# Twenty-four gate projections spread over four stages, and the third triangular solve moved into the scan

## The chip, the core and the metric

The kernel runs on one core of a Trainium2 chip. A core has a matrix engine (TensorE, PE in the profile; its weight loads are PEld), a vector engine (VectorE, DVE), an activation engine (ScalarE, ACT), a general engine (GpSimd, POOL) and a queue that issues most transfers (SyncE, SP). Each engine works through its own list of instructions in order, and semaphores make one wait for another. The metric is the time on the device in microseconds (us) for one launch. The kernel before takes 1673.54 us, the median of three runs (1671.61 to 1678.89).

## The reference

One layer of a hybrid backbone on 512 latent and 256 context tokens of width 1024, all in float32. One input projection `w_in` feeds three token mixers; their outputs are weighted by gates, projected and followed by a convolutional feed-forward part. What matters here:

```python
proj = h @ w_in      # split into q/k/v, z, a/b, hyena, lru x, lru y, gates
# A. gated DeltaNet: 8 heads, chunks of 64 tokens, two directions
t_inv = triangular_solve(eye + m, eye, left_side=True, lower=True)
def step(state, inp):                      # 4 context chunks, then 8 latent ones
    v_new = u_i - w_i @ state
    o_i = q_i @ state + a_i @ v_new
    state = state * d_i + k_i @ v_new
o = rms_norm(o, norm_g) * silu(z)          # z: 8 column blocks of proj
# B. Hyena (long convolution), C. RG-LRU, 8 blocks of 128 channels, two directions
r = sigmoid(blockdiag(x, w_a) + b_a); i = sigmoid(blockdiag(x, w_x) + b_x)
log_a = -8 * r * softplus(-lam)
h = linear_scan(exp(log_a), sqrt(-expm1(2 * log_a)) * (i * x), h0)
out = (h_f + flip(h_b)) * gelu(p_y)
# merge: three sets of 8 gate blocks
g_dn, g_hy, g_lru = split(sigmoid(p_gate))
merged = g_dn * (o_dn @ w_proj_dn) + g_hy * (o_hy @ w_proj_hy) + g_lru * (o_lru @ w_proj_lru)
```

The z blocks and the three sets of gates are 32 equal projections of the latent tokens, 1024 x 128 weights each. Their results are kept in DRAM until they are needed, so 24 of them (z, g_dn, g_hy; kinds 0, 1 and 2 in the kernel) can be computed anywhere between the normalised input and the work behind the scan.

## The kernel before

Every float32 product that matters is done as three products of rounded parts. `load_w` (L165) loads a 128 x 1024 weight tile (L168), splits it into a high part (L157 on POOL or L155 on ACT) and a low part (L160 on DVE or POOL), and `mm3` (L172 to L175) issues three matmuls for each of eight slices of the width. A gate on 512 tokens is thus 24 matmuls of 128x512, a sigmoid or silu on ACT (L574) and a store to the DRAM tensor `gated` (L575). Loads and stores share SP's queue.

The program has these stages, with their times in the trace of before:

- *RG-LRU* (101 to 340 us): eight blocks `g`. Each has the projection of the next block's input (`lru_in`, with the copies and the short convolution on L484 to L487), the eight small gate products and their sigmoids (`lru_gates`, L518 and L519 on ACT, L520 on DVE), four tanhs (L524, L525), one gate of kind 3, `lru_decay` (two exponentials L532 on ACT; L534 on DVE, L535 on POOL, a square L536 on ACT, L537 on DVE, a square root L539 on ACT), `lru_scan` (L542 to L547 on DVE), `lru_y` (a projection, L555 to L558), and `lru_out`, which adds and multiplies on POOL (L562, L563) and splits the result with L155 on ACT. Sigmoid and tanh, the exponential and the square root are in different tables of ACT, so ACT loads a table (ACT_TABLE_LOAD) where the function changes.
- *Merges, queries* (340 to 447): `lru_merge(h)` for seven values of h, each a projection of the RG-LRU output times a gate, between the DeltaNet's queries. Then the keys and the chunks' Gram matrices (447 to 540).
- *First two solves* (540 to 650): each `solve` inverts triangular blocks. Two transposes prepare its buffers (L819); an inner loop of 31 steps, two DVE instructions each (L827, L829), solves 32x32 blocks; transposes (L837, L839) put them back; 32x32 matmuls on TensorE (L853, L857) with copies on ACT complete the 64x64 inverses; the results go to the DRAM tensor `wad`. `run` weaves the two solves' steps with a work list of values and gates in turn, one item every third step.
- *Third solve* (650 to 743): `solve_second`, for the chunks that the scan reaches from its step 7 on, woven with the rest of the list.
- *Scan* (743 to 948): twelve steps, four on context and eight on latent chunks. A step loads its chunk (v, `wa`, kd), multiplies the state (L1005), subtracts (L1009), applies the inverse (L1015), and updates the state (L1023, L1028); between a step's two parts and behind it stands a gap. Half a gate goes into each of the 24 gaps. After some steps `mod_part` multiplies a tile of `w_mod` on DVE (L1052, L1054), and `mod_sum` sums it up.
- *Rest* (948 to 1675): Hyena, output projections, feed-forward.

A list scheduler orders each engine's instructions from the program, with the items under `tc.high_priority()` ahead. The order of an engine is therefore not always the order of the code.

Of the kernel before, what the change touches and what calls it, by code (L numbers as in the profile page):

```python
# [17 lines left out]
P = 128  # L18
# [55 lines left out]
def tile_block(ctx: ExitStack, tc: tile.TileContext, I: dict, out: bass.AP, dbg=None, upto=99):  # L74
    nc = tc.nc
# [496 lines left out]
    def gate_store(z_, m, pg):  # L572
        th = ur([P, NL])
        act(th, pg, GATES[z_][1])  # L574
        load(gated[z_, m], th)  # L575
# [25 lines left out]
    NFILL = 12  # L601
# [28 lines left out]
    for g in range(8):  # L630
# [4 lines left out]
        gate(3, g)  # L635
        lru_decay([g], [bufs])
# [89 lines left out]
    for h in range(1, NH):  # L726
        lru_merge(h)
        if h < 6:
            sqs.append(query(h + 2))
        if h < 7:  # L730
            query_out(h, sqs[h])
        if h > 1:
            for i, d in pairs[2 * h - 4:2 * h - 2]:
                decays(i, d)
# [76 lines left out]
    def solve(dirs, M, NX_, tmr, eng):  # L811
# [31 lines left out]
        for half in range(2):  # L843
            zp = dn([P, 16, 32])
            rp = dn([P, 16, 32])
            for c in range(2):
# [3 lines left out]
                ci = slice((1 - d) * 32, (1 - d) * 32 + 32)  # L850
                for a in range(16):
                    e = half * 16 + a
                    mmul(zp[pi, a, :], M[pj, e, ci], Wu[pj, e, :], start=True, stop=True)  # L853
                act(Z[pi, half * 512:half * 512 + 512], zp[pi].rearrange("p a b -> p (a b)"), AF.Copy)
                for a in range(16):
# [12 lines left out]
    def solve_second():  # L868
        yield from solve((0, 1), M3.rearrange("p t c h i -> p (t c h) i"),
                         [at(180 + 4 * i, [P, 32, 32]) for i in range(2)], ring(1, seq(188, 1, 2)), "dve")  # L870
# [53 lines left out]
    fill = [(z_, m) for z_ in range(3) for m in range(8)]  # L924
    EVERY, NW1 = 3, 12
# [10 lines left out]
    gates = [lambda f=f: gate(*f, "act", "pool") for f in fill[:NFILL]]  # L936
    work = [w_ for p_ in zip(values, gates) for w_ in p_] + values[len(gates):] + gates[len(values):]
    run([solve_first(0), solve_first(1)], work[:NW1])
    run([solve_second()], work[NW1:])
# [15 lines left out]
    mm = Banks([0])  # L955
    o = at(60, [P, 4, NH, P])
    S = [at(84 + 4 * d, [P, NH, P]) for d in range(2)]
    war = ring(4, seq(92, 4, 4))
# [6 lines left out]
    def chunk_loads(s, lat):  # L965

        v, kd, wa = vr([P, NH, P]), kdr([P, NH, P]), war([P, 2 if lat else 1, NH, 64])
# [88 lines left out]
    def mod_sum(q):  # L1056
        if q in (1, 2):
            mp = mm([P, 8])
# [3 lines left out]
        else:  # L1062
            row, brow = wr([1, D]), wr([1, D])
            load(brow, I["b_mod"][:, (2 + q) * D:(3 + q) * D])
            for b in range(2):
                mp = mm([1, 512])
# [4 lines left out]
    def gate_halves(z_, m):  # L1071
# [4 lines left out]
        gate_store(z_, m, pg)  # L1076
# [3 lines left out]
    halves = (None for z_, m in fill[NFILL:] for _ in gate_halves(z_, m))  # L1080
    ngap, FBM = 2 * (24 - NFILL), 1
    gap = 0
    for s_ in range(12):
# [3 lines left out]
        for part, _ in enumerate(step(s_)):  # L1087
            gap += 1
            for _ in range(gap * ngap // 24 - (gap - 1) * ngap // 24):
                next(halves)  # L1090
        for k in range(4) if s_ % 3 < 2 else ():
            mod_part(s_ // 3, s_ % 3 * 4 + k)
    assert next(halves, 1) == 1
# [515 lines left out]
```

## Time and profile before

| | us |
|---|---|
| runs of before (median of three) | 1671.61 / 1673.54 / 1678.89 |
| the profiled execution | 1676.85 |
| its span, first to last instruction | 1675.1 |
| TensorE busy | 1529.7 (91%) |
| DVE busy | 1195.7 (71%) |
| ACT busy | 615.7 (37%) |
| POOL busy | 589.3 (35%) |

The profile is of one execution; the page gives its busy times, a row of 40 slices of the span, the queues and the costliest groups of instructions. The trace behind it is asked for stretches of time (busy time of each engine, granted TensorE clock, DMA share), timelines (each instruction with the idle time before it and what ended it), waits and lines. A granted clock of 1.00 is the upper level of TensorE, 2.4 GHz, and 0.50 the lower, 1.2 GHz. In a stage, what counts is the wait that ends last there; a busy share over the whole span is a mean over stages with different limits.

### The profile page before, as it was taken

What the parts mean: (1) busy time and instruction counts of PE and PEld (TensorE: products, weight loads), DVE (VectorE), ACT (ScalarE), POOL (GpSimd) and SP (SyncE); (2) the same over time, 40 slices, a digit from 0 to 9 for tenths busy, and PEclk for the clock granted to TensorE, in tenths of its full rate; (3) what the DMA queues carried; (4) which work ended last, traced back from release to release, by engine and by line L of the source; (5) the groups of instructions that cost most, each with busy time, mean ns of one, the idle gap of its engine ahead of it and who ended that gap; (6) DMA issues with size and microseconds to landing.
All of it is one profiled execution on the core that took longest, in us unless ns stands there. A gap on an engine that the chain in (4) does not pass through costs nothing. (4 is left out here: it accounts for less than half of the span.)

```text
span 1675.1 us, 23659 instructions
## 1 busy us (share of the span) xinstructions
PE 1529.7 (91%) x9176; PEld 1258.0 (75%) x9176; DVE 1195.7 (71%) x1752; ACT 615.7 (37%) x1011; POOL 589.3 (35%) x401
## 2 busy tenths in 40 slices
PE   6899888889999899887999889999999999999998
PEld 2677777767887777775788678787888788888876
DVE  6877888756656997834666375777766899989873
ACT  4367787734553232320111330333222433333311
POOL 4653534325444360312434114222321233334441
PEclk9899999999999896878899999999999999999999
DMA  9432222335344332577888736322462223232331
GB/s 343 162 107 82 76 76 81 103 104 175 127 126 125 110 101 74 173 211 206 233 227 244 253 109 231 107 88 84 162 207 64 68 96 97 92 101 98 104 113 50
DMA packets 93056, 225.66 MB, mean 135 GB/s; under 512 B 9963, under 2 KB 30699, under 8 KB 92176
## 3 DMA queue, kind: packets, MB, share of 16 engines
q1 hardware_dynamic: 92112, 217.86, 41.6%
q0 software_dynamic: 832, 6.29, 0.9%
q8 instruction: 72, 1.18, 0.3%
q14 instruction: 40, 0.33, 0.1%
HBM read 190.45 MB, written 33.66 MB: 134 GB/s over the span
## 5 line engine op out<-in xcount | busy, mean ns | idle before, releaser
L173 PE MATMUL bank<-region,region 128*128 128x512 f32 (+1 forms) x2032 | 761.8, 376 | 28.9 <-DVE region L487 6.8
L175 PE MATMUL bank<-region,region 128*128 128x512 f32 (+1 forms) x2032 | 755.2, 373 | 25.1 <-DVE region L160 22.1
L174 PE MATMUL bank<-region,region 128*128 128x512 f32 (+1 forms) x2032 | 757.2, 373 | 4.2 <-DVE region L160 2.1
L173 PEld LDWEIGHTS bank<-region,region 128*128 128x128 f32 x2032 | 389.7, 192 | 106.8 <-ACT region L155 10.4
L175 PEld LDWEIGHTS bank<-region,region 128*128 128x128 f32 x2032 | 389.5, 192 | 98.6 <-DVE region L160 28.6
L174 PEld LDWEIGHTS bank<-region,region 128*128 128x128 f32 x2032 | 390.6, 192 | 69.0 <-DVE region L418 4.4
L160 DVE TENSOR_TENSOR region<-region,region 128x1024 fp32r<-128x1024 f32 (+2 forms) x241 | 268.7, 1128 | 174.1 <-ACT region L155 98.2
L155 ACT ACTIVATE region<-region 128x1024 fp32r<-128x1024 f32 (+2 forms) x209 | 178.4, 865 | 422.9 <-PE bank L174 132.8
L160 POOL TENSOR_TENSOR region<-region,region 128x1024 fp32r<-128x1024 f32 (+1 forms) x64 | 157.3, 2463 | 237.9 <-ACT region L155 200.4
L157 POOL TENSOR_SCALAR region<-region 128x1024 fp32r<-128x1024 f32 (+1 forms) x96 | 114.3, 1193 | 330.4 <-PE bank L174 147.7
L1423 DVE SCALAR_TENSOR_TENSOR region<-bank,pc,region 128x441 f32<-128x441 f32 (+2 forms) x352 | 224.8, 688 | 4.3 <-ACT region L1412 0.7
L485 DVE SCALAR_TENSOR_TENSOR region<-bank,pc,region 128x511 f32<-128x511 f32 (+1 forms) x56 | 34.1, 629 | 48.7 <-ACT region L482 45.8
L1054 DVE SCALAR_TENSOR_TENSOR region<-region,cc,region 128x1024 f32<-128x1024 f32 x28 | 41.7, 1488 | 33.9 <-DMA region<-in_w_mod_dram 33.4
L992 POOL TENSOR_TENSOR region<-region,region 128x512 f32<-128x512 f32 x32 | 49.1, 1564 | 39.5 <-DMA region<-rowd 36.8
L482 ACT ACTIVATE region<-bank,pc 128x512 f32<-128x512 f32 (+1 forms) x40 | 23.1, 597 | 98.6 <-PE bank L175 98.6
L1435 POOL TENSOR_TENSOR region<-region,region 128x512 f32<-128x512 f32 x22 | 34.3, 1561 | 66.3 <-DVE region L1423 52.3
L1028 DVE SCALAR_TENSOR_TENSOR region<-region,egl,bank 128x128 f32<-128x128 f32 x160 | 42.3, 339 | 21.3 <-PE bank L1023 21.3
L1005 PE MATMUL bank<-region,region 128*64 128x128 f32 x608 | 42.4, 306 | 9.2 <-DVE region L1028 9.2
L1005 PEld LDWEIGHTS bank<-region,region 128*64 128x64 f32 x608 | 39.8, 157 | 14.4 <-DVE region L1028 6.4
L1017 ACT ACTIVATE region<-bank 128x512 f32<-128x512 f32 x24 | 14.3, 598 | 89.9 <-PE bank L1015 89.9
L574 ACT ACTIVATE region<-bank 128x512 f32<-128x512 f32 x32 | 18.8, 588 | 70.6 <-PE bank L175 66.4
L1137 POOL TENSOR_TENSOR region<-region,region 128x512 f32<-128x512 f32 x8 | 12.2, 1523 | 85.6 <-DVE region L1121 85.6
(275 smaller groups left out, 1669.7 us busy)
## 6 DMA issues: line engine op xcount, KB each, us to landing
region<-in_w_in_dram SPq DMA_DIRECT2D x97, 512.0 KB, 3.9
region<-in_w_mod_dram SPq DMA_DIRECT2D x48, 512.0 KB, 6.2
region<-in_ffn_up_dram SPq DMA_DIRECT2D x44, 512.0 KB, 3.5
region<-in_w_proj_dram SPq DMA_DIRECT2D x24, 512.0 KB, 3.6
region<-in_ffn_down_dram SPq DMA_DIRECT2D x22, 512.0 KB, 3.5
gated<-region SPq DMA_DIRECT2D x32, 256.0 KB, 2.1
region<-gated SPq DMA_DIRECT2D x32, 256.0 KB, 4.0
kdd<-region SPq DMA_DIRECT2D x16, 384.0 KB, 2.8
```

The lines of the kernel that those rows point to most:

```text
L155: act(hi, raw, AF.Copy)
L157: nc.gpsimd.tensor_scalar(hi, raw, 1.0, 0.0, op0=ALU.mult, op1=ALU.add)
L160: (vtt if e_lo == "dve" else gtt)(lo, raw, hi.bitcast(F32), op=ALU.subtract)
L173: mmul(ps, lh, rh, start=start, stop=False)
L174: mmul(ps, lh, rl, start=False, stop=False)
L175: mmul(ps, ll, rh, start=False, stop=stop)
L992: gtt(wq[d][:, hs], KQ[hf][:, :, chs[d] - 4], eg[:, hs].unsqueeze(2).to_broadcast([P, 4, 2, 64]), op=ALU.mult)
L1005: mmul(X[hf][rcs[d], h, :], wq[d][:, hf * 4 + h, kind], S[d][:, hf * 4 + h, :], start=(kind == 0 or h == 0), stop=(kind == 0))
L1028: stt(S[d][:, h], S[d][:, h], egl[:, d, c, i, h:h + 1], p3[hf][d][:, h % 4], op0=ALU.mult, op1=ALU.add)
L1054: stt(acc, w_, cc[:, k, 0:1], acc, op0=ALU.mult, op1=ALU.add)
L1423: stt(uv[:, ro, co], pv_[:, ri, ci], w[:, a * 3 + b:a * 3 + b + 1], uv[:, ro, co], op0=ALU.mult, op1=ALU.add)
L1435: gtt(uu[0], uu[0], uu[1], op=ALU.mult)
```

## The change

Of the 24 gates of kinds 0 to 2, before computes 12 woven with the solves and 12 in the scan (two halves each, one half in each gap). After:

- eight stand in the RG-LRU blocks, one in each, right behind the gate of kind 3, with both splits on POOL (`NEARLY = 8`);
- six stand in the merge loop, behind `lru_merge(h)`, with the high split on ACT and the low one on POOL (`NMERGE = 6`);
- five stand beside the two first solves, behind all nine items of the values (`NSOLVE = 5`);
- five stand in the scan, as ten halves over 24 gaps; their results are stored over ACT's queue in place of SP's.

The list of gates begins with kind 1, then 0, then 2. `solve_second` no longer has a stage of its own: it is started in front of the scan and advanced in the scan's gaps, four steps in a gap up to step 3 and one step in a gap from then on. For this its last part gets another pause, its buffers move, the ring for `wa` has two slots up to step 6 and four from step 7 on, the solve's and `mod_sum`'s PSUM banks are set apart, and lines after L573 shift by 3 to 12 (the scan's L1009, L1015, L1028, L1054 are L1017, L1023, L1036, L1062 after; the inner loop L827, L829 is L834, L836; the solve's transposes L837, L839 are L844, L846).

```diff
-    def gate_store(z_, m, pg):
+    def gate_store(z_, m, pg, store=load):
         th = ur([P, NL])
         act(th, pg, GATES[z_][1])
-        load(gated[z_, m], th)
+        store(gated[z_, m], th)
...
-    NFILL = 12
+    NEARLY, NMERGE, NSOLVE = 8, 6, 5
+    NBEF = NEARLY + NMERGE + NSOLVE
+    fill = [(z_, m) for z_ in (1, 0, 2) for m in range(8)]
...
         gate(3, g)
+        if g < NEARLY:
+            gate(*fill[g], "pool", "pool")
         lru_decay([g], [bufs])
...
         lru_merge(h)
+        if h <= NMERGE:
+            gate(*fill[NEARLY + h - 1], "act", "pool")
...
                     mmul(zp[pi, a, :], M[pj, e, ci], Wu[pj, e, :], start=True, stop=True)
                 act(Z[pi, half * 512:half * 512 + 512], zp[pi].rearrange("p a b -> p (a b)"), AF.Copy)
+            yield
+            for pj, pi, ci in blocks:
                 for a in range(16):
...
-    gates = [lambda f=f: gate(*f, "act", "pool") for f in fill[:NFILL]]
-    work = [w_ for p_ in zip(values, gates) for w_ in p_] + values[len(gates):] + gates[len(values):]
-    run([solve_first(0), solve_first(1)], work[:NW1])
-    run([solve_second()], work[NW1:])
+    run([solve_first(0), solve_first(1)], values + [lambda f=f: gate(*f, "act", "pool") for f in fill[NBEF - NSOLVE:NBEF]])
...
-    mm = Banks([0])
+    dn = Banks([6, 7])
+    mm, mm1 = Banks([0]), Banks([1])
...
-    war = ring(4, seq(92, 4, 4))
+    wars = [ring(4, [92, 96]), ring(4, [100, 104, 92, 96])]
...
-        gate_store(z_, m, pg)
+        gate_store(z_, m, pg, nc.scalar.dma_start)
...
-    halves = (None for z_, m in fill[NFILL:] for _ in gate_halves(z_, m))
-    ngap, FBM = 2 * (24 - NFILL), 1
+    later = solve_second()
+    next(later)
+    halves = (None for z_, m in fill[NBEF:] for _ in gate_halves(z_, m))
+    ngap, FBM = 2 * (24 - NBEF), 1
...
                 next(halves)
+            for _ in range(4 if s_ < 4 else 1):
+                next(later, None)
```

How the instructions stand, at two places. First ACT in an RG-LRU block, before. `region_106` is the high part of the RG-LRU output (so this L155 is `lru_out`'s), `region_1065` to `region_1068` are the next block's buffers, `bank_...` a result of TensorE:

```order
L524 ACTIVATE region_1067<-region_1065,sp_745 128x768
L155 ACTIVATE region_106<-region_1353 128x512
L525 ACTIVATE region_1068<-region_1065,sp_744 128x768
L574 ACTIVATE region_1491<-bank_63 128x512
L532 ACT_TABLE_LOAD
L532 ACTIVATE region_1065<-region_1065,nsp_746 128x768 x2
L555 ACTIVATE region_992<-bank_64 128x512
L557 ACT_TABLE_LOAD
```

Before, `lru_out`'s split stands behind the next block's sigmoids and three of its tanhs, and one table load stands between it and the exponentials (the pair L532 x2).

ACT in an RG-LRU block after, from the same split on (`region_882` to `region_885` are the block's buffers here):

```order
L155 ACTIVATE region_106<-region_1234 128x512
L519 ACTIVATE region_883<-bank_69,pc 128x512
L518 ACTIVATE region_882<-bank_70,pc 128x256
L519 ACTIVATE region_882<-bank_67,pc 128x512
L518 ACTIVATE region_883<-bank_70,pc 128x256
L519 ACTIVATE region_883<-bank_68,pc 128x512
L524 ACTIVATE region_884<-region_882,sp_745 128x768
L155 ACTIVATE region_860<-region_86 128x768
L525 ACTIVATE region_885<-region_882,sp_744 128x768
```

After it come one more L524 and L525, and then the exponentials with the gates' sigmoids among them:

```order
L532 ACT_TABLE_LOAD
L532 ACTIVATE region_882<-region_882,nsp_746 128x768
L574 ACT_TABLE_LOAD
L574 ACTIVATE region_950<-bank_65 128x512
L532 ACT_TABLE_LOAD
L532 ACTIVATE region_882<-region_882,nsp_746 128x768
L574 ACT_TABLE_LOAD
L574 ACTIVATE region_980<-bank_66 128x512
L536 ACTIVATE region_884<-region_882 128x1536
```

The split now stands ahead of five sigmoids (L518, L519) and all the tanhs, and two gates' sigmoids with their table loads stand among the exponentials and the square.

Second, DVE around the first subtractions of the scan, before (`region_5395` is the accumulator of the modulation, `region_5391` a state):

```order
L1054 SCALAR_TENSOR_TENSOR region_5395<-region_436,cc,region_5395 128x1024
L1054 SCALAR_TENSOR_TENSOR region_5395<-region_696,cc,region_5395 128x1024
L1054 SCALAR_TENSOR_TENSOR region_5395<-region_878,cc,region_5395 128x1024
L1009 TENSOR_TENSOR region_1354<-region_5479,bank_65 128x512
L160 TENSOR_TENSOR region_698<-region_878,region_697 128x1024
L1009 TENSOR_TENSOR region_2456<-region_5479,bank_66 128x512
L1028 SCALAR_TENSOR_TENSOR region_5391<-region_5391,egl,bank_69 128x128 x4
```

The same place after (`region_5380` is the accumulator, `region_5382` the third solve's solution, `region_5415` and `region_5418` its temporaries):

```order
L836 TENSOR_TENSOR region_5382<-region_5382,region_5415 128x9x23
L1062 SCALAR_TENSOR_TENSOR region_5380<-region_436,cc,region_5380 128x1024
L834 TENSOR_TENSOR region_5418<-region_5381,region_5382 128x192
L1062 SCALAR_TENSOR_TENSOR region_5380<-region_696,cc,region_5380 128x1024
L1017 TENSOR_TENSOR region_1442<-region_5461,bank_65 128x512
L1062 SCALAR_TENSOR_TENSOR region_5380<-region_878,cc,region_5380 128x1024
L1017 TENSOR_TENSOR region_2688<-region_5461,bank_66 128x512
L836 TENSOR_TENSOR region_5382<-region_5382,region_5418 128x8x24
L834 TENSOR_TENSOR region_5415<-region_5381,region_5382 128x175
L836 TENSOR_TENSOR region_5382<-region_5382,region_5415 128x7x25
```

Step 1's subtractions now stand among the inner loop of the third solve: 47 of its 62 instructions are ahead of the pair on DVE and 15 behind, and the state's update (L1036) comes after those.

## Rows read from the trace of the kernel before

**Rows 1.** The page: busy time by engine; TensorE's granted clock in tenths.

```profile
PE 1529.7 (91%) x9176; PEld 1258.0 (75%) x9176; DVE 1195.7 (71%) x1752; ACT 615.7 (37%) x1011; POOL 589.3 (35%) x401
...
PEclk9899999999999896878899999999999999999999
```

**Rows 2.** Seven stretches: busy us by engine, granted clock, DMA share, GB/s.

```profile
101.00:340.00 239.00, 213.26 (x1043) 173.66 (x1042) 189.74 (x196) 179.24 (x229) 89.83 (x59) 1.00 0.26 82
340.00:447.00 107.00, 100.09 (x487) 82.62 (x488) 61.52 (x92) 44.81 (x69) 43.86 (x39) 0.97 0.45 141
447.00:540.00 93.00, 88.69 (x638) 73.44 (x638) 55.17 (x112) 43.39 (x144) 42.35 (x29) 1.00 0.41 119
540.00:650.00 110.00, 96.40 (x720) 80.73 (x715) 106.91 (x194) 32.42 (x51) 43.23 (x13) 0.91 0.33 105
650.00:743.00 93.00, 81.98 (x722) 69.98 (x720) 52.56 (x84) 25.49 (x40) 21.14 (x14) 0.76 0.54 160
743.00:811.00 68.00, 52.76 (x452) 41.68 (x452) 36.80 (x70) 9.23 (x16) 15.84 (x14) 0.87 0.76 212
811.00:948.00 137.00, 130.47 (x1465) 110.76 (x1466) 79.55 (x167) 18.84 (x33) 50.39 (x35) 0.95 0.83 228
```

**Rows 3.** ACT timeline, one RG-LRU block: start, duration, operation, [idle before].

```profile
207.21 0.63 ACT L155 ACTIVATE region<-region 128x512 fp32r<-128x512 f32 x1 [4.19 <-POOL region L563]
...
209.18 1.28 ACT L532 ACT_TABLE_LOAD   x1
...
210.47 1.77 ACT L532 ACTIVATE region<-region,nsp 128x768 f32<-128x768 f32 x2
...
223.07 1.26 ACT L519 ACTIVATE region<-bank,pc 128x512 f32<-128x512 f32 x2
...
226.08 0.97 ACT L524 ACTIVATE region<-region,sp 128x768 f32<-128x768 f32 x1
...
228.66 0.92 ACT L525 ACTIVATE region<-region,sp 128x768 f32<-128x768 f32 x1
...
229.48 0.92 ACT L524 ACTIVATE region<-region,sp 128x768 f32<-128x768 f32 x1
...
234.61 0.63 ACT L155 ACTIVATE region<-region 128x512 fp32r<-128x512 f32 x1 [4.20 <-POOL region L563]
```

**Rows 4.** Who waited for line 563: us, times.

```profile
  ACT region L155: 34.6, 8
```

**Rows 5.** TensorE timeline, two matmuls ten apart in one gate.

```profile
204.68 0.39 PE L175 MATMUL bank<-region,region 128*128 128x512 f32 x1
...
206.95 0.39 PE L173 MATMUL bank<-region,region 128*128 128x512 f32 x1
```

**Rows 6.** TensorE timeline, the scan's first matmul.

```profile
743.35 0.66 PE L1015 MATMUL bank<-region,region 64*64 64x128 f32 x2 [5.51 <-DMA region<-vd]
```

**Rows 7.** DVE timeline, the end of the first two solves.

```profile
647.63 1.88 DVE L839 STREAM_TRANSPOSE region<-region 32x1024 f32<-32x1024 f32 x1
```

**Rows 8.** Busy us and granted clock in 25 us of the solves' matmuls.

```profile
650.00:675.00 25.00, 25.00 (x252) 21.25 (x251) 9.38 (x27) 4.12 (x7) 1.42 (x2) 0.50 0.25 86
```

**Rows 9.** POOL timeline beside the first two solves.

```profile
572.27 2.39 POOL L160 TENSOR_TENSOR region<-region,region 128x1024 fp32r<-128x1024 f32 x1 [6.21 <-ACT region L155]
...
582.95 13.91 POOL L160 TENSOR_TENSOR region<-region,region 128x1024 fp32r<-128x1024 f32 x2 [8.29 <-ACT region L155]
```

**Rows 10.** DVE timeline, inner loop of the third solve.

```profile
692.45 2.40 DVE L829 TENSOR_TENSOR region<-region,region 128x156 f32<-128x156 f32 x1
...
695.22 0.30 DVE L829 TENSOR_TENSOR region<-region,region 128x135 f32<-128x135 f32 x1
```

**Rows 11.** Groups of DVE's instructions, 649 to 726 us.

```profile
L829 DVE TENSOR_TENSOR region<-region,region 128x31 f32<-128x31 f32 (+15 forms) x31 | 13.6, 438 | 1.0
L827 DVE TENSOR_TENSOR region<-region,region 128x31 f32<-128x31 f32 (+15 forms) x31 | 13.2, 427 | 1.1
```

**Rows 12.** The page's group of line 1054: busy, mean ns, idle before and releaser.

```profile
L1054 DVE SCALAR_TENSOR_TENSOR region<-region,cc,region 128x1024 f32<-128x1024 f32 x28 | 41.7, 1488 | 33.9 <-DMA region<-in_w_mod_dram 33.4
```

More of the change, by code (lines that the diff above doesn't have):

```diff
@@ L845, in solve @@
             rp = dn([P, 16, 32])
+            blocks = []
             for c in range(2):
@@ L850, in solve @@
                 ci = slice((1 - d) * 32, (1 - d) * 32 + 32)
+                blocks.append((pj, pi, ci))
                 for a in range(16):
@@ L869, in solve_second @@
         yield from solve((0, 1), M3.rearrange("p t c h i -> p (t c h) i"),
-                         [at(180 + 4 * i, [P, 32, 32]) for i in range(2)], ring(1, seq(188, 1, 2)), "dve")
+                         [at(68 + 4 * i, [P, 32, 32]) for i in range(2)], ring(1, seq(64, 1, 2)), "dve")
         for d in range(2):
@@ L922, in run @@
                 each.pop(0)()
-    fill = [(z_, m) for z_ in range(3) for m in range(8)]
-    EVERY, NW1 = 3, 12
+    EVERY = 3
     vss = {}
@@ L965, in chunk_loads @@
     def chunk_loads(s, lat):
-        v, kd, wa = vr([P, NH, P]), kdr([P, NH, P]), war([P, 2 if lat else 1, NH, 64])
+        v, kd, wa = vr([P, NH, P]), kdr([P, NH, P]), wars[s >= 7]([P, 2 if lat else 1, NH, 64])
         for d in range(2):
@@ L1057, in mod_sum @@
         if q in (1, 2):
-            mp = mm([P, 8])
+            mp = mm1([P, 8])
             for b in range(8):
@@ L1065, in mod_sum @@
             for b in range(2):
-                mp = mm([1, 512])
+                mp = mm1([1, 512])
                 mmul(mp, ones[:, 0:1], acc[:, b * 512:(b + 1) * 512], start=True, stop=True)
@@ L1090, in tile_block @@
                 next(halves)
+            for _ in range(4 if s_ < 4 else 1):
+                next(later, None)
         for k in range(4) if s_ % 3 < 2 else ():
             mod_part(s_ // 3, s_ % 3 * 4 + k)
-    assert next(halves, 1) == 1
+    assert next(halves, 1) == 1 and next(later, 1) == 1
     in_order((ET.PE,))
```

## The prediction

> **What bounds the kernel now.** I read the page's first two parts first: TensorE is busy 91% of the span, and in its clock row a few slices stand at 6 to 8 tenths [rows 1]. So all the gates' matmuls are paid somewhere in any case, and only two things can change the time: idle TensorE, and TensorE at its lower level. The table by stage [rows 2] says where these are. In the RG-LRU stage (101 to 340 us) TensorE works 213.26 of 239.00 us at full clock: 25.7 us idle, the largest loss outside the scan. In the merges (340 to 447) it works 100.09 of 107.00: 6.9 us idle. In the two stretches with solves (540 to 743) it works 178.4 of 203, but the granted clock is 0.91 and 0.76. In the scan (743 to 948) it works 183.2 of 205.
>
> What matters next is *why* TensorE is idle in the RG-LRU stage. In the ACT timeline of one block the hi half of the block's output (L155) starts at 207.21 after 4.19 us of idleness that POOL's L563 ended, and the next block's at 234.61 after 4.20 us [rows 3]; ACT waits for L563 8 times, 34.6 us in all [rows 4]. The period is 234.61 - 207.21 = 27.4 us. Walked through, the block is a loop: lru_out's L155, then on ACT the two exponentials, then DVE and POOL in turn, the square root, the scans, L562, L563, and again L155. Nobody on that loop has slack; TensorE, whose matmuls of one block come to 213.26 / 239 x 27.4 = 24.4 us, waits for the loop. So the stage is bound by a latency loop through ACT, not by TensorE, and idle TensorE there is not free room unless the loop stays as short as it is.
>
> **The change, part by part.** A gate is 24 matmuls. Ten of them start within 206.95 - 204.68 = 2.27 us [rows 5], so a gate is 24 x 0.227 = 5.45 us of TensorE at full clock, wherever it stands.
>
> *Eight gates into the RG-LRU stage.* Matmuls: 8 x 5.45 = 43.6 us. If TensorE were the bound, 25.7 us would go into idle time and the stage would grow by 43.6 - 25.7 = 18 us. But the order on ACT also moves. Before, between lru_out's L155 and DVE's L534 stand one tanh, one sigmoid, one table load and two exponentials: 207.21 to 212.27, 5.06 us (the exponentials start at 210.47 and take 1.77) [rows 3]. After, that L155 stands ahead of five gate sigmoids of the block, four tanhs and a weight split; the added gate's sigmoid splits the two exponentials, which makes three table loads where there was one. Priced by spacing in [rows 3]: L155 0.55; five sigmoids 2.4 (the six from 223.07 to 226.08 take 3.0); four tanhs and a split 4.1 (0.82 each, 228.66 to 229.48); three loads of 1.28, two exponentials of 0.88 and a sigmoid of 0.6 are 6.2. Together 13.3 us, 8.2 more. Two things shorten the loop: the load ahead of the square root comes while DVE still works (-1.3), and a convolution and splits leave the place between DVE's scans (0 to -2.2). The loop becomes 27.4 + 4.7 to 6.9; I take 32.4, the end nearer to TensorE's own 24.4 + 5.45 = 29.9 us. Eight blocks: +40 us, with ends +18 (TensorE alone) and +55 (8 x 6.9). POOL's two more splits per block are free: it is busy 89.83 of 239 us.
>
> *Six gates into the merges.* 6 x 5.45 = 32.7 us where 6.9 are idle, and these idle pieces are waits that a gate ahead of them partly fills. +34 us, ends +31 and +40.
>
> *Solves.* Seven gates (38.2 us) and the third solve's 32x32 matmuls (about 12 us) leave 540 to 743. TensorE's work there falls from 178.4 to 128, so it can end at 668; with the 13.6 us idle that 540 to 650 has now, 682; with the 5.51 us in which the scan's first matmul waits for a DMA behind the solve [rows 6], 688. DVE agrees: it is saturated (106.91 of 110 us [rows 2]) and has the two first solves until 649.5 [rows 7]; two more values' convolutions come before that end (some 3.4 us each), so 656, and then the matmul tail. That tail stays at the lower level as it does now: 25.00 us busy at a granted 0.50, the 1.2 GHz level, in 650 to 675 [rows 8]. The scan starts at about 690 in place of 743.35: -53 us, ends -45 and -62. What is late next is the store of the solved blocks and the load that follows it, on SP's queue, now behind the last gates' stores.
>
> *Scan.* Seven fewer gates in halves, plus the third solve's 12 us: TensorE's work falls from 183.2 to 157, and with the 21.8 us idle of now that is 179 against 205. The transfers say the same: 212 x 68 + 228 x 137 is 45.6 MB; seven gates take away 0.75 MB each (a weight and a store), the third solve's store and load add 0.5: 40.9 MB, at 228 GB/s 179 us. -26 us, ends 0 (a new wait takes all of it) and -36 (170 us, were the mean 240 GB/s, which I set by hand). The second ring of two slots for the solved blocks delays no step below seven, since a load then has a whole step to land.
>
> Sum: +40 + 34 - 53 - 26 = -5 us on the profiled 1676.85, so about 1671.9. That execution lies 3.3 us over the median 1673.54, and so I predict 1668.5.
>
> **A rule to weigh.** POOL's low split L160 takes 2.39 us at 572.27, but two of them from 582.95 take 13.91 [rows 9], while DVE runs the solves' inner loop; and one L829 of the inner loop takes 2.40 us at 692.45 where a slightly smaller one just after takes 0.30 [rows 10]. So each engine stretches the other's instruction here. The Trainium skill, page "SBUF — State Buffer", section "Who interferes with whom", says that a DVE instruction with two inputs in SBUF contends with a GpSimd instruction that reads SBUF. By that rule, which the trace bears out in these rows, POOL splits beside the third solve, now in the scan, and beside the first two would cost more than the sum above holds; what they cost is the third rival.
>
> **The rivals.**
> *A, the gates in the RG-LRU stage are nearly free* (the loop overlaps between blocks more than I walk it, and TensorE becomes the bound): +18 there in place of +40, so -27: about 1646.5. For it: TensorE already works 89% of the stage. Against: ACT's eight waits for L563, without exception.
>
> *B, slower: DVE's queue at the scan's start.* The third solve's inner loop costs DVE 13.6 + 13.2 = 26.8 us [rows 11], and DVE is in order: 47 of its 62 instructions, among them the largest, some 22 us, and eight partial sums of the modulation (1.49 us each [rows 12], 11.9 together) stand ahead of step 1's subtraction L1017, 15 more ahead of its state update. Between the end of the first solves on DVE (656) and the scan's start (690) there are 34 us, just what these need. If the partial sums' weights come late (DVE now waits 33.4 us for them, by the same row) or the first solves end late, step 1 waits, and the first four steps last as long as now plus the remainder of the solve: scan -4 in place of -26, so +17: about 1690. It decides from some 10 us of lateness of L1017 on.
>
> *C, slower: POOL and DVE.* The pair from 582.95 lost 9.1 us, and TensorE's 13.6 us idle in 540 to 650, with two such pairs in it, make at most 6 to 7 for each. Two or three more, as the consecutive values and the scan's gates run beside inner loops, cost 16 us: about 1684.5.
>
> **How the numbers follow.** Forecast 0.45, with its own range 1657 to 1680; A 0.24; B 0.20; C 0.11. A measurement of this kernel can tell 0.5%, 8.4 us. Faster by more than that (below 1665.2): 0.4 of the forecast's, nearly all of A's, 0.42 in all. Slower (above 1681.9): little of the forecast's, most of B's and C's, 0.27. Within: 0.31. The range reaches A's and B's values, 1643 to 1691.
>
> **What would show it.** In the new profile: the distance between the L155s that wait for lru_out's POOL product is 32 us and not 30 (A) nor 34; the RG-LRU stage ends near 380; ACT has six table loads per block; the merges last 141 us; the scan's first L1023 (the old L1015) starts near 764 in its own time (743.35 + 40 + 34 - 53); the scan lasts 175 to 182 us and DVE's first L1017 doesn't keep TensorE for more than a few us. If the stage's blocks stand 30 us apart, the loop was no bound and the step on ACT fails. If a half clock spreads into the scan's first steps, because TensorE has fewer full-size matmuls there, the forecast is too low.

## The result: slower, and the net miss lies in the scan

The changed kernel takes 1707.31 us, the median of four runs (1700.26 to 1708.70); before, measured with it, takes 1674.68. The ratio is 1.0162, 95% interval [1.0134, 1.0190]: slower by 1.6%, clear of noise. The profiled execution took 1708.56 us, its span is 1706.8 us. The forecast was 1668.5 with a range of 1643 to 1691.

Where the two traces part, by the starts of the instructions named (us):

| | before | after | difference added | forecast |
|---|---|---|---|---|
| last L563 (RG-LRU) | 339.4 | 376.6 | +37.2 | +40 |
| first transposed key (merges done) | 447.7 | 529.4 | +44.5 | +34 |
| scan's first L1015 / L1023 | 743.4 | 762.3 | -62.8 | -53 |
| scan's last L1035 / L1043 | 947.5 | 979.0 | +12.6 | -26 |
| end | 1675.1 | 1706.8 | +0.2 | 0 |

Up to the scan the sum was forecast as +21 and is +18.9: the first L1023 was to start near 764 and starts at 762.3. That this sum came so near is luck: the merges took 10.5 us more than forecast and the solves 9.8 us less. The scan was to last 179 us and lasts 217. The same table as in [rows 2], for after, with its own borders (busy us of TensorE, its weight loads, DVE, ACT, POOL; granted clock; DMA share; GB/s):

```profile
101.00:377.00 276.00, 256.13 (x1209) 212.06 (x1210) 193.02 (x193) 200.62 (x248) 119.74 (x73) 0.96 0.28 92
377.00:529.00 152.00, 144.12 (x657) 118.34 (x656) 64.19 (x94) 59.41 (x87) 60.87 (x46) 0.94 0.42 134
529.00:653.00 124.00, 114.66 (x803) 96.24 (x802) 83.93 (x146) 53.68 (x161) 48.05 (x32) 1.00 0.39 117
653.00:762.00 109.00, 92.62 (x843) 77.30 (x842) 102.04 (x209) 32.75 (x52) 30.15 (x11) 0.86 0.44 132
762.00:830.00 68.00, 47.81 (x558) 38.61 (x560) 59.74 (x106) 9.81 (x17) 17.72 (x17) 0.88 0.82 215
830.00:979.00 149.00, 119.81 (x1450) 105.71 (x1446) 69.60 (x158) 19.51 (x32) 38.54 (x32) 0.80 0.74 195
```

Read two things in it. In the scan's second part TensorE is busy 119.8 of 149 us and at a clock of 0.80, where [rows 2] have 130.47 of 137 at 0.95: TensorE waits more, and does its work more slowly. And the transfers go at 195 GB/s where they went at 228. The whole scan of before, and that of after:

```profile
743.40:947.50 204.10, 182.69 (x1914) 152.04 (x1916) 116.04 (x234) 27.76 (x47) 66.23 (x49) 0.92 0.81 222
762.30:979.00 216.70, 167.59 (x2004) 144.27 (x2004) 129.04 (x264) 29.32 (x49) 56.26 (x49) 0.82 0.77 201
```

TensorE's idle time is 204.1 - 182.7 = 21.4 us before and 216.7 - 167.6 = 49.1 us after. By the starts of the steps' first L1015 / L1023 the first four steps take 73.5 us before and 61.1 after, the last eight 130.6 before and 155.6 after: the loss is in steps 4 to 11.

ACT in one RG-LRU block of after, to be held against [rows 3]:

```profile
244.73 0.63 ACT L155 ACTIVATE region<-region 128x512 fp32r<-128x512 f32 x1 [6.03 <-POOL region L563]
...
251.87 1.28 ACT L532 ACT_TABLE_LOAD   x1
253.17 0.94 ACT L532 ACTIVATE region<-region,nsp 128x768 f32<-128x768 f32 x1
254.12 1.28 ACT L574 ACT_TABLE_LOAD   x1
255.42 0.60 ACT L574 ACTIVATE region<-bank 128x512 f32<-128x512 f32 x1
256.03 1.28 ACT L532 ACT_TABLE_LOAD   x1
257.33 0.94 ACT L532 ACTIVATE region<-region,nsp 128x768 f32<-128x768 f32 x1
...
277.79 0.63 ACT L155 ACTIVATE region<-region 128x512 fp32r<-128x512 f32 x1 [5.82 <-POOL region L563]
```

The block's period is 277.79 - 244.73 = 33.06 us, between the two ends of the forecast (32.1 and 34.3), and ACT works without a pause from `lru_out`'s split to the end of the second exponential, 13.5 us, where the walk had 13.3.

TensorE from the first L1023 of step 4 to that of step 5, after:

```profile
823.38 1.96 PE L1023 MATMUL bank<-region,region 64*64 64x128 f32 x32
825.28 1.19 PE L862 MATMUL bank<-region,region 32*32 32x32 f32 x32
827.15 1.40 PE L862 MATMUL bank<-region,region 32*32 32x32 f32 x32 [0.68 <-ACT region L863]
829.22 3.78 PE L1031 MATMUL bank<-region,region 64*128 64x128 f32 x32 [0.68 <-ACT region L863]
...
838.64 1.19 PE L868 MATMUL bank<-region,region 32*32 32x32 f32 x32
840.51 1.19 PE L868 MATMUL bank<-region,region 32*32 32x32 f32 x32 [0.68 <-ACT region L869]
841.64 3.57 PE L1068 MATMUL bank<-ones,region 128*128 128x1 f32 x16
845.14 5.29 PE L1013 MATMUL bank<-region,region 128*64 128x128 f32 x64
850.36 1.96 PE L1023 MATMUL bank<-region,region 64*64 64x128 f32 x32
```

The third solve's matmuls (L862, L868) stand on TensorE between the step's own, each pair with a hop over ACT, and behind them L1031 takes 3.78 us (2.06 elsewhere) and L1013 5.29 (3.71 elsewhere). This step takes 27.0 us; before, the same one takes 19.6. And a stretch of SP's queue, at the end of the scan:

```profile
958.15 0.33 SPq L168 DMA_DIRECT2D region<-in_w_in_dram  x1
958.53 0.45 SPq L981 DMA_DIRECT2D region<-kdd  x1
959.07 0.53 SPq L995 DMA_DIRECT2D region<-rowd  x1
962.83 0.33 SPq L168 DMA_DIRECT2D region<-in_w_in_dram  x1
963.21 0.28 SPq L1077 DMA_DIRECT2D modr<-region  x1
963.59 0.33 SPq L995 DMA_DIRECT2D region<-rowd  x1
```

The last step's second load of decay rows (`rowd`) leaves at 963.59, behind two weight loads and a store that wait for DVE. The state was ready at 958.4, and L1013 ends at 975.5, some 13 us later than the state alone would let it (with 3.71 us for the product). Summed over steps 4 to 11, the step's product with the state (L1013, called W below) ends 42 us later than that in after, 20 us in before, by the ends of L1036 and L1013 in each step. So I had two suspects for the scan: the solve's work in the steps, and late loads.

### The profile page after: what moved, and what is told of

Same layout as the page of the kernel before. It is cut to its first block, busy times and chain, and to the rows that moved or that the text cites. A ratio compares the mean times of both kernels' runs of the same rounds, so it can differ in the third digit from the quotient of the medians.

```text
span 1706.8 us, 23685 instructions
## 1 busy us (share of the span) xinstructions
PE 1541.1 (90%) x9176; PEld 1273.3 (75%) x9176; DVE 1186.0 (69%) x1745; ACT 637.4 (37%) x1027; POOL 596.1 (35%) x409
## 3 DMA queue, kind: packets, MB, share of 16 engines
q1 hardware_dynamic: 91392, 216.55, 40.7%
## 5 line engine op out<-in xcount | busy, mean ns | idle before, releaser
L160 DVE TENSOR_TENSOR region<-region,region 128x1024 fp32r<-128x1024 f32 (+1 forms) x234 | 263.6, 1137 | 195.4 <-ACT region L155 100.0
L155 ACT ACTIVATE region<-region 128x1024 fp32r<-128x1024 f32 (+2 forms) x208 | 177.5, 865 | 443.5 <-PE bank L174 134.9
L160 POOL TENSOR_TENSOR region<-region,region 128x1024 fp32r<-128x1024 f32 (+1 forms) x71 | 172.3, 2430 | 244.0 <-ACT region L155 210.9
L1013 PE MATMUL bank<-region,region 128*64 128x128 f32 x608 | 50.6, 334 | 25.2 <-DVE region L1036 13.2
L1000 POOL TENSOR_TENSOR region<-region,region 128x512 f32<-128x512 f32 x32 | 40.8, 1300 | 89.0 <-DMA region<-rowd 70.9
L1013 PEld LDWEIGHTS bank<-region,region 128*64 128x64 f32 x608 | 46.7, 175 | 31.7 <-POOL region L1000 21.9
L1025 ACT ACTIVATE region<-bank 128x512 f32<-128x512 f32 x24 | 14.3, 597 | 143.5 <-PE bank L1023 132.3
L1447 POOL TENSOR_TENSOR region<-region,region 128x512 f32<-128x512 f32 x22 | 34.3, 1560 | 66.4 <-DVE region L1435 59.6
L1036 DVE SCALAR_TENSOR_TENSOR region<-region,egl,bank 128x128 f32<-128x128 f32 x160 | 42.3, 341 | 20.9 <-PE bank L1031 20.9
L485 DVE SCALAR_TENSOR_TENSOR region<-bank,pc,region 128x511 f32<-128x511 f32 (+1 forms) x56 | 34.3, 627 | 28.8 <-ACT region L482 28.3
L1062 DVE SCALAR_TENSOR_TENSOR region<-region,cc,region 128x1024 f32<-128x1024 f32 x28 | 38.0, 1357 | 17.5 <-DMA region<-in_w_mod_dram 17.2
L1149 POOL TENSOR_TENSOR region<-region,region 128x512 f32<-128x512 f32 x8 | 10.7, 1342 | 84.5 <-DVE region L1133 84.5
L534 DVE SCALAR_TENSOR_TENSOR region<-region,region 128x1536 f32<-128x1536 f32 x8 | 14.8, 1854 | 36.5 <-ACT region L532 36.5
```

The source lines that it names most:

```text
L155: act(hi, raw, AF.Copy)
L160: (vtt if e_lo == "dve" else gtt)(lo, raw, hi.bitcast(F32), op=ALU.subtract)
L485: stt(o[:, off + 1:off + n], ps[:, 0:n - 1], w[:, 0:1], o[:, off + 1:off + n], op0=ALU.mult, op1=ALU.add)
L1000: gtt(wq[d][:, hs], KQ[hf][:, :, chs[d] - 4], eg[:, hs].unsqueeze(2).to_broadcast([P, 4, 2, 64]), op=ALU.mult)
L1013: mmul(X[hf][rcs[d], h, :], wq[d][:, hf * 4 + h, kind], S[d][:, hf * 4 + h, :], start=(kind == 0 or h == 0), stop=(kind == 0))
L1036: stt(S[d][:, h], S[d][:, h], egl[:, d, c, i, h:h + 1], p3[hf][d][:, h % 4], op0=ALU.mult, op1=ALU.add)
```

## The experiments

Times are medians; the ratio is to before on the same chip. "Scan" is from the start of its first L1023 to that of its last L1043, in the profiled run. The diffs are abridged: a name such as `five_gates` or a phrase stands for longer code.

**Third solve ahead of the scan in the program.**

```diff
-    run([solve_first(0), solve_first(1)], values + five_gates)
+    run([solve_first(0), solve_first(1)], values)
+    run([solve_second()], five_gates)
...
-    later = solve_second(); next(later)
+    later = iter(())
```

> The changed kernel with the third solve put back into a stage of its own ahead of the scan, the five gates beside it; the scan keeps only five gates. The scan (first to last matmul of a step) took 204 us before and 217 us after. Theory S (the third solve among the scan's steps makes them long, by its matmuls, its DVE loop and its stores): the scan falls to 178-188 us, and the total stays near 1700, since a stage of some 60 us is added and 27 us of gates leave the first two solves. Rival F (the scan is long because it has too few full-size matmuls, so TensorE falls to its lower level and steps wait for loads): the scan stays at 200-215 us, and the total is 1720-1740.

1703.28 us, 1.0122 [1.0087, 1.0157]; scan 208.6. The total is near S's and the scan lies in F's range, but not for F's reason: the scheduler put step 0 ahead of the end of the solve, and TensorE then stood behind it:

```profile
PE bank L862 <- DVE region L846: 18.8, 2, 17.0
```

(TensorE's waits from 759 to 806 us: total, times, longest.) From step 0 to step 1 it takes 44.9 us, but steps 1 to 11 take 160.2 us, where after takes 201.6. So steps 1 to 11 are some 40 us shorter without the solve among them; but their loads also had the 33 us by which step 0 is longer to run ahead, and this run can't tell the two apart.

**No gates in the RG-LRU stage, thirteen in the scan** (`NEARLY = 0`).

> The changed kernel with the eight gates of the RG-LRU stage moved into the scan (thirteen there, as 26 halves over 24 gaps). Theory L (the scan's steps are a chain of waits, for loads, the third solve and the state, with idle TensorE in it): the RG-LRU stage gets back its 37 us, the scan grows by at most 15 us, total 1670-1685. Rival P (TensorE's work is the scan's bound): the scan grows by 8 x 5.45 = 44 us, total 1708-1715.

1686.82 us, 1.0055 [1.0025, 1.0084]. Theory L holds in direction: the RG-LRU stage is back at 338.9, the scan takes 235.8 us, 19 more for 43.6 us of matmuls. Its 15 us were too few.

**Decay rows over ACT's queue.**

```diff
-            load(eg, rowd[1, d, chs[d]].partition_broadcast(P))
+            nc.scalar.dma_start(eg, rowd[1, d, chs[d]].partition_broadcast(P))
```

> The changed kernel with one edit: the scan's loads of the decay rows (rowd) are issued on ACT's queue and no longer on SP's, where they stand behind stores and modulation weights that wait. Theory Q (order on SP's queue makes these loads late): POOL's waits for rowd in the scan fall from 98 us to under 50, the scan from 217 to about 195-203 us, total 1685-1693. Rival D (they are late because the transfers themselves are slow, or other waits bound the steps): scan 212-220 us, total 1703-1711.

1705.23 us, 1.0142 [1.0105, 1.0180]; scan 211.4. POOL's waits for rowd did fall, to 10 us, and steps 7 to 11 took 65 us in place of 90. But ACT, in order as well, now waited 67 us for POOL to free the buffers, and TensorE for ACT; steps 1 to 7 became 20 us longer. Loads moved in the order, and the scan hardly got shorter; the total is rival D's.

**The added RG-LRU gates by a copy, then both gates by a copy** (kinds 3 and the added one; their outputs aren't the gates').

> The changed kernel with the eight added gates of the RG-LRU stage evaluated by a copy in place of a sigmoid (their values are wrong, the work on TensorE, POOL and SP is the same), so that ACT has no table to load for them. Theory A (the stage's loop through ACT sets its period, and the two loads among the exponentials are on it): the period of a block falls from 33.0 to about 30.5 us, the stage by 15-20 us, total about 1690. Rival T (TensorE's 29.9 us and its own waits set the period): 32.5-33 us, total 1704-1708.

1707.95 us (two runs), 1.0153 [1.0088, 1.0217]; the period stayed at 33.1. The edit took away the wrong load: the sigmoid between the exponentials is kind 3's, and the added gate's falls into the time in which ACT waits for POOL anyway. The wait grew by about what the load had taken (1.28 us), from 2.40 us in after to

```profile
261.95 1.49 ACT L536 ACTIVATE region<-region 128x1536 f32<-128x1536 f32 x1 [3.82 <-POOL region L535]
```

> The changed kernel with both gates of each RG-LRU block (kind 3 and the added one) evaluated by a copy (values wrong), so that no table load stands between the two exponentials or behind them. Theory A (the loop through ACT sets the period): two loads of 1.28 us leave the loop, the period falls from 33.05 to 30.5 us. Rival T (TensorE sets it): 32.5-33.1 us.

1691.42 us (one run). The period fell to 31.2 to 31.4 us, not to 30.5; the stage ends at 363.5 in place of 376.6. The two splits of `lru_out` that ACT waits for:

```profile
236.13 0.63 ACT L155 ACTIVATE region<-region 128x512 fp32r<-128x512 f32 x1 [1.97 <-POOL region L563]
...
267.51 0.63 ACT L155 ACTIVATE region<-region 128x512 fp32r<-128x512 f32 x1 [0.50 <-POOL region L563]
```

The loop through ACT did set the period; the wait of ACT for L563 shrinks from 6 us to 2.0 in one block and 0.5 in the next, and from there on something else holds it. Its scan, with after's code, took 210.8 us: between runs this scan varies from 211 to 217 (215.4 in the run before this one).

**The third solve's matmuls made wide** (four of 32x512 for each of the two kinds; the solve's values change).

> The changed kernel with the 128 + 128 small 32x32 matmuls that end the third solve replaced by 8 wide ones of 32x512 (its values are wrong; its loop on DVE, its copies on ACT, its stores and all loads stay). Theory Z (these small matmuls, in the gaps of steps 4 and 5, lengthen the steps by their own time, the lower TensorE level that they bring and the two hops through ACT): from step 4's first L1023 to step 6's it takes 30-36 us in place of 50.6, the scan falls from 217 to 198-205, total 1690-1697. Rival Q2 (late loads of the decay rows set these steps too): 46-51 us, scan 212-217, total 1703-1710.

1703.79 us, 1.0141 [1.0120, 1.0163]; scan 210.9, steps 4 to 6 43.8 us, against 44.8 in the run just named. It settles nothing on Z: a wide one takes 1.04 us where the sixteen small ones that it replaces take 1.19, so that hardly any time was taken away, and the total is that of Q2.

**Without the last part of the third solve, and without the solve but for its stores.**

```diff
-        for half in range(2):
+        for half in range(2 if last else 0):      # first run: last=False for the third solve
...
-        yield from solve((0, 1), M3..., "dve")
+        for _ in range(37):                       # second run
+            yield
```

> The changed kernel with the last part of the third solve left out (its matmuls L862 and L868 and their copies on ACT; values wrong); its loop and transposes on DVE and its stores stay. In the trace after, that part stands in TensorE's order between the steps' own matmuls, 7 us in each of steps 4 and 5, and TensorE is at its lower level behind it. Theory Z2 (it stands on the steps' chain): from step 4's first L1023 to step 6's 28-34 us in place of 50.6 (44.8 to 50.6 in runs with the same scan code), the scan 190-198, total 1682-1692. Rival Q2 (the loads of the decay rows come too late for these steps, whatever TensorE does): 42-50 us, scan 208-217.

1700.81 us, 1.0115 [1.0080, 1.0150]; scan 210.6. Step 5 fell to 12.4 us, but step 4 stayed at 28.3: there TensorE now waited 7.22 us for DVE's modulation sums and then for POOL's product with the decay rows. The step lost one cause and kept its length. From step 4's first L1023 to step 6's it takes 40.7 us, in neither range; the scan is in Q2's.

> The changed kernel without the third solve, but for its stores to wad (values wrong). Against the one without its last part alone this takes away the loop and the transposes on DVE. Theory J (the loop on DVE delays steps 1 to 3 and the start): from step 1's first L1023 to step 4's 42-45 us in place of 49, scan 3-8 us shorter than without the last part, total 1675-1685. Rival: nothing, since DVE has the room: 0 us. If the late steps (7 to 11) still take 110 us and more, the late loads of the decay rows there have another cause than the solve's work.

1688.76 us, 1.0053 [1.0033, 1.0073]; scan 201.3. Steps 1 to 3 took 45.4 us (48.4 in the run without the last part alone, 49.5 in after): J holds in direction, just outside its ranges, and the total is 12 us under that run's. Steps 7 to 11 take 84.7 us (90.0 in after), under the 110 of the expectation's last condition, so that it doesn't apply. With all the solve's arithmetic gone the scan is still 20 us longer than with the solve ahead of it (next), and W is 45 us late over steps 4 to 11.

**Other splits of the gates with the solve ahead of the scan**: eleven gates in the scan and five beside the solves; seven and nine; both with none in the merges.

> The third solve put ahead of the scan's steps in the program, eight gates in the RG-LRU stage, none in the merges, five beside the solves, eleven in the scan. Theory M (a gate in the merges costs its full TensorE time and more, 44.5 us for six, and one in the scan 2.4 to 3 us): the merges take 108 us, the scan 222-230, total 1674-1684. Rival P2 (a gate costs about 5.45 us in the scan as well): scan 241, total 1690-1695.

> As the one with none in the merges and eleven in the scan, but with nine gates beside the solves and seven in the scan. Theory M and S together (the four gates fill TensorE's 17 us of waiting for the third solve's transposes): total 1668-1680. Rival P2: 1690-1695.

Eleven: 1695.96 us, 1.0097 [1.0058, 1.0136]; the merges are short again (114 us), but step 0 takes 47.9 us, as in the first experiment, and the scan 230.8. Seven: 1682.07 us, 1.0015 [0.9991, 1.0039]; here the solve's last matmul starts at 766.9 and the scan at 772.5: scan 181.1 us, near the 179 that were forecast for five gates. Both totals lie above theory M's ranges.

```profile
772.50:953.60 181.10, 152.60 (x1794) 129.17 (x1796) 103.88 (x228) 24.77 (x42) 55.49 (x45) 0.91 0.85 223
```

Its first four steps take 60.0 us, about as in after (61.1); its last eight 121.1, where after takes 155.6.

**Gates of the RG-LRU blocks behind `lru_y`**, on top of that version.

```diff
-        gate(3, g); gate(*fill[g], "pool", "pool")
         lru_decay([g], [bufs]); lru_scan(*bufs)
         y, u = lru_y(g)
+        gate(3, g); gate(*fill[g], "pool", "pool")
```

> The version with the third solve ahead of the scan, no gate in the merges, nine beside the solves and seven in the scan, and with one more edit: in each RG-LRU block both gates stand behind the projection lru_y, so that their sigmoids share a table load with its sigmoid and none stands between the exponentials. Theory A (the loop through ACT sets the period, 33.1 us): the period falls to 29.9-31 us, the stage by 17-25 us, total 1657-1667, under the kernel before. Rival T (waits for the splits and TensorE's own time take the loop's place): 32-33 us, total 1677-1683.

1678.14 us, 0.9991 [0.9974, 1.0008]: no difference from before. ACT has four table loads again, and yet the period is 32.1 to 33.7 us: rival T. It is the best of the versions with gates in that stage, and doesn't beat before.

**High priority for the decay rows' loads**, in after, in the kernel without the solve's last part, in before, and in the version just told.

> The changed kernel with one edit: the loads of the decay rows get the scheduler's high priority, so that on SP's queue they stand ahead of the modulation's and the next stage's weights (the last step's pair no longer behind two weight loads and a store). Theory Q (order on SP makes W wait in steps 5, 8, 10 and 11): the product W ends within 2 us of the state's update in these steps, where the sum over steps 4 to 11 was 42 us, now under 25; scan 190-202 us where the changed kernel has 211-217; total 1683-1695. Rival B (the transfers' bandwidth delays them wherever they stand in the queue): sum 35-45 us, scan 208-217, total 1700-1710.

> The same edit in the kernel without the last part of the third solve (values wrong). Theory Q and Z2 together: what the scan has over 180 us is these two; scan 178-188 us, total 1670-1682. If they are one delay seen twice (the late rows hide behind the solve's matmuls), only one of them shows: scan 195-205.

> The kernel before with the same edit of the priority alone (third solve in its stage, 24 half gates in the scan). In before W ends 20 us later than the state's update allows, summed over steps 4 to 11. Theory Q: 5-12 us of them go, scan 192-199 in place of 204, total 1663-1671. Rival B: scan 202-206, total 1673-1680.

> The version with the third solve in its own stage, no gate in the merges and the late gates in the RG-LRU blocks, with the edit of the priority. Its scan is 181-185 us with 16 us of lateness. Theory Q: scan 175-180, total 1668-1674. Rival B: 1675-1680.

None of Q's forecasts came out; the first run alone has rival B's time and scan. 1708.47 us, 1.0172 [1.0141, 1.0202]; 1713.44, 1.0199 [1.0150, 1.0247]; 1697.96, 1.0104 [1.0066, 1.0142]; 1696.19, 1.0103 [1.0060, 1.0145]. In after W's lateness fell from 42 to 22 us, as Q had it, but the scan stayed at 208.5. In before the scan grew from 204.1 to 222.7 us by the order of one kind of load alone; SP now stands 46.4 us in front of a buffer that POOL still uses (SP's waits in its scan):

```profile
SPq L988 <- POOL region L993: 46.4, 12, 10.1
```

So late rows alone are not the cause. Put side by side, the scans differ in their transfers (packets and MB over the scan of before, of after, and of the version with the solve ahead and seven gates):

```profile
DMA packets 14866, 45.39 MB, mean 222 GB/s; under 512 B 2066, under 2 KB 2066, under 8 KB 14684
```

```profile
DMA packets 14601, 43.57 MB, mean 201 GB/s; under 512 B 2037, under 2 KB 2037, under 8 KB 14425
```

```profile
DMA packets 13066, 40.39 MB, mean 223 GB/s; under 512 B 1848, under 2 KB 1848, under 8 KB 12876
```

Up to here every scan with the solve or its stores among the steps moved 191 to 209 GB/s, whether it held five or thirteen gates. Two scans without them are no faster, before and the version just told, each with the priority: 205 and 202 GB/s. And the bytes alone don't set the length: the changed kernel with the priority, with the solve's last part and without it, moves 40.9 and 39.9 MB in 208.5 and 209.1 us, the version with the solve ahead and seven gates 40.4 MB in 181.1.

**Half of the modulation's weights**, in after and in before.

```diff
-        load(w_, I["w_mod"][rows_k, cols_q])
-        stt(acc, w_, cc[:, k, 0:1], acc, op0=ALU.mult, op1=ALU.add)
+        load(w_[:, 0:512], I["w_mod"][rows_k, first 512 of cols_q])
+        for b in range(2):        # the same half twice
+            stt(acc_half_b, w_[:, 0:512], cc[:, k, 0:1], acc_half_b, op0=ALU.mult, op1=ALU.add)
```

> The changed kernel with half of each modulation weight loaded in the scan (512 of 1024 columns, used twice; values wrong), so that DVE does the same work in two halves and some 7 MB of the scan's 43.6 MB aren't transferred. Theory R (the scan lasts as long as its transfers through SP's queue need, 201 GB/s in the changed kernel): 36.5 MB at about 203 GB/s, scan 178-188 us, total 1668-1682. Rival C (the chain of the steps on TensorE, DVE and POOL sets it, transfers follow): scan 205-215, total 1698-1708.

> The same edit in the kernel before: 6.5 MB of 45.4 less. Theory R there too: 38.9 MB at 222 GB/s, scan 175-180 us. Rival P (before has TensorE as the bound, busy 182.7 of 204 us, so that transfers hide): scan 192-202 us, total 1665-1678.

In after 1679.91 us, 1.0002 [0.9981, 1.0023]; its scan:

```profile
761.50:947.10 185.60, 153.79 (x2004) 133.09 (x2004) 141.90 (x290) 29.22 (x49) 59.09 (x49) 0.89 0.73 189
```

185.6 us where R said 178 to 188, 31 us less than after, with the solve, its matmuls and its loop all left as they were, and DVE busier (141.9 against 129.0). R's two factors both missed, though: 35.0 MB went at 189 GB/s, the lowest rate of all these scans, and at R's 203 GB/s they would have taken 173 us. Nor is it the bytes alone that changed: the scheduler put SP's queue into another order. The last step's two loads of decay rows now leave together, ahead of the weight load and the store that stood before the second one (rows from 958.15 on, above):

```profile
920.53 0.35 SPq L168 DMA_DIRECT2D region<-in_w_in_dram  x1
...
922.11 1.00 SPq L995 DMA_DIRECT2D region<-rowd  x2
927.33 0.33 SPq L168 DMA_DIRECT2D region<-in_w_in_dram  x1
```

SP's waits in front of the modulation's loads (L1058) fall from 75 to 49 us, TensorE's idle time from 49.1 to 31.8. TensorE's busy time fell too, from 167.6 to 153.8, for the same 2004 matmuls: the clock rose from 0.82 to 0.89. W's lateness over steps 4 to 11 is down to 20 us. Nearly all of the gain is in these steps: 122.1 us in place of 155.6. In before 1677.08 us, 1.0000 [0.9984, 1.0015]; scan 198.4 us, 6 us less for 7.8 MB: rival P, within its range. So the modulation's loads cost after's scan most of its excess and before's scan little; whether by their bytes, or by the order and the waits of the queue that they stand in, this edit doesn't separate.

## Why the prediction was wrong, step by step

*RG-LRU, +40: right in size, by the loop that it named.* +37.2 measured, period 33.06. That ACT's loop set it is shown by the run with both gates copied (33.1 to 31.3 us); that the block then meets another limit at once is shown by that run and by the late gates (32.1 to 33.7 us). The sum's end of +18 was not near: without the eight gates the merges are done at 483.0 in place of 529.4, so the gates cost 46.4 us up to there, no less than their full 43.6 us of matmuls.

*Merges, +34: mis-sized, +44.5 measured, beyond the end of +40.* Without gates in the RG-LRU stage the same six cost 35.8 us (483.0 - 338.9 against 447.7 - 339.4), so some 9 us come with the RG-LRU gates; how they get there was not followed up. Over both stages TensorE's idle time went only from 32.7 to 27.8 us, and its busy time grew by 86.6 us for 76.3 us of gates, the clock falling from 0.99 to 0.96.

*Solves, -53: mis-sized, -62.8.* The two first solves took their gates with less stretched POOL splits than in [rows 9]: the longest is 5.1 us, where the pair there has 13.91. Rival C found nothing there. Which term of the sum was 10 us too large was not followed up.

*Scan, -26: this step failed, and decides the result.* It is +12.6, 38.6 us off. The prediction added up TensorE's work, 157 us, and "the 21.8 us idle of now". Measured are 167.6 us of work, since the clock was 0.82 and not 0.92, and 49.1 us of idle time: +10.6 and +27.3. So what failed is that the idle time of before's scan, and its clock, were carried over to a scan with other work in it; nothing in the sum held the waits that came with it. The second sum, "the transfers say the same ... 40.9 MB, at 228 GB/s 179 us", failed with it. The bytes: 43.57 MB, since loads that before had done during the third solve's stage (decay rows, modulation weights, and the solve's stores) now fall into the scan; at 228 GB/s that is 191 us, 12 more. The rate: 201 GB/s, and 43.57 MB at that rate are 217 us, 26 more. This second factor is the scan's length over again, as a rate is bytes over time, and names no cause. I took over the rate of a scan in which every load had a solve's stage to run ahead; that this head start is what was lost fits the run with the solve done ahead (181.1 us) and the one with its stores alone (201.3), but no run varied it by itself. That the modulation's loads are on the way is shown by the run with 8.5 MB less, which is 31 us shorter; since its queue has another order too, it doesn't show that the bytes are the reason. How a late load becomes a long step is seen in the rows above: SP, POOL and DVE each stand in order behind whatever comes late, and mending one of these (ACT's queue, the priority) moves the wait to the next.

*The rivals.* A (nearly free gates in the RG-LRU stage) is refuted by the period. B, "DVE's queue at the scan's start", named the right stage and sign, but not the mechanism: TensorE waited 2.7 us for step 1's L1017, and steps 0 to 3, which B had as long as before or longer, took 61.1 us in after and 73.5 in before. The prediction's sign that a lower clock would come in the first steps came later: 0.88 there, 0.80 behind. The solve's arithmetic is worth about 10 to 15 us of the scan (the run with its stores alone), its matmuls little when taken alone. What remains open is the cause of the other waits of steps 4 to 11: the order on SP can lengthen a scan alone, as before with the priority shows (222.7 us at 205 GB/s), but no run with the solve among the steps and all its bytes brought 222 GB/s back.

## What to carry to other kernels

A stage's time is at least the larger of several budgets, with the waits on top, and each of them needs its own check when work moves in: for the scan the bytes were counted, but those of the stage that was removed ahead of it, in which loads had run ahead, were not. Taking a stage away takes its transfer time away too. Idle time and rate are results of a stage's waits and no constants of it: here scans of 40 to 41 MB took 181 to 209 us. And idle time of an engine in a stage that a loop of waits sets is not room, as [rows 3] and the run without these gates show: eight gates put into 25.7 us of idle TensorE cost 46.4 us, no less than their 43.6 us of matmuls.

## What the runs showed of the hardware

A short wait can go with a lower granted clock, and need not: in two of three RG-LRU blocks of after one idle gap of 2.5 us goes with 0.95 over the block (0.69 over the 5.5 us around the gap), while the third block, with a gap of 2.3 us, shows 1.00, as a block of before with three gaps of 0.6 to 1.6 us does. In the scan the same 2004 matmuls took 167.6 us of TensorE at 0.82 and 153.8 us at 0.89. Behind the third solve's small matmuls L1031 stood at the lower level (3.78 us, at 0.50); behind wide ones of 32x512 too (3.55 us, at 0.51); without either it took 2.06 us at 1.00. Making those matmuls wide, with the waits for ACT between them left, did not bring the clock back.
